# First mixer: a stacked low-rank product for the decays, and GpSimd for the weights' remainders

## The chip, the cores and the metric

One core of one Trainium2 chip runs the whole program in one launch. The metric is device microseconds of that core, the median of the runs shown. A core has five engines with queues of their own: TensorE (PE, with its weight loads as PEld), VectorE (DVE), ScalarE (ACT), GpSimd (POOL) and SyncE (SP, which issues most of the loads here). Within one queue, instructions start in order; a wait at the head of a queue holds all that stand behind it.

## The reference: what is computed

Two layers of a hybrid backbone over 768 tokens (512 latent and 256 context tokens) of width 1024, in float32. The change touches the first layer's mixer only, and there two things: the forget gates of the gated linear attention (GLA), and how projection weights are prepared.

```python
gq, gk, gv, gog, gz, aq, ak, av = _split(h @ w_in, EVEN_SIZES)   # gz: 32 columns, two directions of rank 16
...
for d, z in enumerate(jnp.split(gz, 2, axis=-1)):
    logit = (z @ gla_w_gate[d] + gla_b_gate[d]).astype(jnp.float32)
    g = _heads(jax.nn.log_sigmoid(logit) / GLA_GATE_TAU, GLA_HEADS)
    dirs.append(_directional_scan(q, k, v, g, n_ctx, reverse=(d == 1)))
```

For each direction, 16 columns of `gz` times a 16 x 256 matrix give 256 logits per token; their log-sigmoid is the log of the decay.

## The kernel before, in words

**How a product keeps float32 accuracy.** A matmul on plain float32 operands runs in several passes over the array, one on operands rounded to `fp32r` runs in one. The kernel therefore writes a large product X W as a sum of three one-pass products, with X = XH + XL and W = WH + WL (rounded part and remainder): `mm3` (line 812) issues H·H, H·L and L·H. ACT rounds a weight tile (`nc.scalar.copy`, line 803), and DVE makes its remainder, `raw - H` (line 804). Both stand in `split`, the inner function of `fetched` (lines 794 to 807), which first puts the load of the raw tile on SP's queue (line 799). The raw tiles have three buffers, `wH` and `wL` four each. `split` has a parameter `vector` for the engine of the subtraction; only the early columns of the first mixer (`weights`, line 2021) pass GpSimd, for tiles of 128 x 576. All others use DVE, in tiles of 128 x 1024. The two large feed-forward stages prepare their weights elsewhere (line 861) and are not touched.

**The first mixer** (`even_mixer`, from line 1115) multiplies the normed tokens by the columns of `w_in` in groups: `qk` (GLA's queries and keys, transposed), `nat` (values, output gates, attention's queries, keys and values), and `z` (the 32 columns of `gz` with 256 columns of attention's queries, computed first). Each of the groups qk0, qk1, v0, v1, q, kv, g0 and g1 loads two weight tiles of 128 x 1024, so there are sixteen of them.

**The decays.** ACT copies the 32 columns of each of six token tiles from PSUM to `zn` (line 1162). The generator `decays` (line 1173) turns them on PE into `zT`, 32 rows by 768 tokens, with a DVE copy out of PSUM (line 1179). `wg` holds both directions' 16 x 256 matrices, one below the other in 32 rows, with zeros elsewhere: a memset on GpSimd and two loads on SP (lines 1167 to 1170). `gla_gates` (line 1276) then does, for each half c of the columns, each token group (context, latent) and each direction, one plain float32 matmul of depth 32 (line 1285), and an Abs, Exp, Ln, min, subtract, Exp sequence on ACT and DVE (lines 1288 to 1293).

**The modulation vectors beside it.** In the same stretch DVE computes two pairs of modulation vectors out of 16 tiles of `mod_w` (`mod_vec`, from line 533): for each tile of 128 x 1024 two multiply-adds into accumulators `macc` (lines 553 and 555), whose loads (line 479) have three buffers of their own on SP's queue. After each half of the tiles PE sums the accumulators over the partitions (`mod_acc`), DVE copies the sums out (line 487), and PE turns them into columns.

**What sets the order.** On PE the order is written out by hand: strings of step names, each of which advances a generator by one step (`run`, line 1252), with the matmuls pinned to that order:

```python
run("qk0 e m qk0 e e v0 qk0 e e m qk0 e e m v0 e e m m q v0 m m v0 m m kv q m q m q m m m m m m m m m m qk1 kv m")
tp.release()
gp = self.open_pool("gla")
run("c0 l0 kv m c0 kv c0 v1 qk1 c0 p p qk1 c0 l0 p qk1 l0 c0 g0 qk1 l0 p c1 p v1 l0 p v1 l0 c1 p v1 l0 c1 l1 g1 g0 c1 g0 r0 c1 l1 r0 g0 l1")
```

Here `e` is `decays`, `m` is `mod_vec`, c0, l0, c1 and l1 are the chunked scans (`scan`, line 947), `p` is attention's normalisation and rotary step (`att_prep`, line 1334, which gives GpSimd a power and two multiplications per token tile, lines 686 and 1382), r0 and r1 the read-outs, x and y attention. The other engines' queues are ordered by the framework's planner, which places an instruction by its own costs when its inputs are due, so that order can shift when an instruction is moved or lengthened. The scans' memory (`gla`) takes the place of `gate`, which holds `zn`, `zT`, `wg`, `macc` and the tiles of `mod_w`; scans start when these are free.

Of the kernel before, what the change touches and what calls it, by code (L numbers as in the profile page):

```python
# [8 lines left out]
F32 = mybir.dt.float32  # L9
F32R = mybir.dt.float32r  # L10
# [3 lines left out]
ALU = mybir.AluOpType  # L14
# [3 lines left out]
P = 128  # L18
# [4 lines left out]
NT = SEQ + CTX  # L23
NTT = NT // P
# [9 lines left out]
class Split:  # L34


    def __init__(self, pool):
        self.pool, self.tiles = pool, None
# [26 lines left out]
class Forms:  # L65
# [29 lines left out]
    def split(self, n, f, i, m):  # L95
        H, L = (x[:, :, i : i + m] for x in self.tiles[n])
        self.net.nc.scalar.copy(H, f)
        self.net.mark = self.net.nc.vector.tensor_tensor(L, f, H.bitcast(F32), op=ALU.subtract)
# [218 lines left out]
class Net:  # L317
# [3 lines left out]
    def __init__(self, ctx, tc, I, out):  # L321
        self.tc, self.nc, self.I, self.out = tc, tc.nc, I, out
        tc.nc.scalar.preload_act_table_set("silu_and_others")
        self.side = 0
        self.whole = False
        self.pinned = False
        self.turns, self.steps, self.pair, self.casts, self.latest = [], [], [], [], []
        pool = lambda name, bufs=1, **k: ctx.enter_context(tc.tile_pool(name=name, bufs=bufs, **k))
        self.cst = pool("cst")
        self.wp = pool("wp")  # L330
        self.sm = pool("sm", 4)
        self.dr = pool("dr", space=bass.MemoryType.DRAM)
        self.ps = None
        self.banks(False)

    def pool(self, name, bufs=1):
        return self.tc.tile_pool(name=name, bufs=bufs, reuse_waits="tile")
# [456 lines left out]
    def fetched(self, src, k, n, raw=None):  # L794

        nc = self.nc
        raw = self.wp.tile([P, WU], F32, tag="raw", bufs=3, name="raw") if raw is None else raw
        m = k * n
        nc.sync.dma_start(out=raw[:, :m].rearrange("p (k n) -> p k n", k=k), in_=src)

        def split(pool=None, to=None, vector=nc.vector):
            H, L = to or [(pool or self.wp).tile([P, WU], F32R, tag=f"w{x}", bufs=4, name=f"w{x}") for x in "HL"]
            self.casts = self.casts[-1:] + [nc.scalar.copy(H[:, :m], raw[:, :m])]  # L803
            vector.tensor_tensor(L[:, :m], raw[:, :m], H[:, :m].bitcast(F32), op=ALU.subtract)  # L804
            return H[:, :m].rearrange("p (k n) -> p k n", k=k), L[:, :m].rearrange("p (k n) -> p k n", k=k)

        return split
# [307 lines left out]
    def even_mixer(self, h, mix, z):  # L1115
        nc, I = self.nc, self.I
# [8 lines left out]
        def q_part(n):  # L1125
            return natq.rearrange("p t (m n e) -> p t m n e", m=4, n=2)[:, :, :, n, :]
# [3 lines left out]
        gqk = [mixg.tile([P, NT], F32, tag=f"gqk{x}", bufs=1, name=f"gqk{2 * x}") for x in range(2)]  # L1130
        og = [p.tile([P, NTT, 256], F32, name=f"og{c}") for c, p in enumerate((mixg, mix))]
        tp = self.open_pool("gate")
        zn = tp.tile([P, NTT, 32], F32, name="zn")
        zT = tp.tile([32, NT], F32, name="zT")

        gq, gk, ends = {}, {}, {}
        def qk(c):
            Ws = {x: self.unit_cols(w, x * P) for x in (c, c + 2)}
            yield
            for x in (c, c + 2):  # L1140
                pt = self.mm_tile(f"gqk{x}")
                for g in groups:
                    self.gemm_T(pt, Ws[x], h, (g,))
                    if g is groups[-1]:
                        t = gqk[x // 2] if c == 0 else mixg.tile([P, NT], F32, tag=f"gqk{x // 2}", bufs=1, name=f"gqk{x}")
                        if x < 2:
                            nc.scalar.mul(t, pt[:, :NT], 0.125)
                            gq[c] = t
                        else:
                            nc.scalar.copy(t, pt[:, :NT])  # L1150
                            gk[c] = t
                    yield

        with self.behind():
            early = qk(0)
            next(early)
        rest = self.late_constants()
        self.pinned = True
        with self.tc.issue_after(self.casts[0].ins):
            for t0 in tiles:  # L1160
                for a, pt in enumerate(z(t0, 3)):
                    nc.scalar.copy(zn[:, t0 + a, :], pt[:, 0:32])
                    nc.scalar.copy(q_part(0)[:, t0 + a], pt[:, 32:288].rearrange("p (m e) -> p m e", m=4))
        self.pinned = False
        rest()

        wg = tp.tile([32, 2, 256], F32, name="wg")
        nc.gpsimd.memset(wg, 0.0)
        for d in range(2):
            nc.sync.dma_start(out=wg[16 * d : 16 * d + 16, d, :], in_=I["gla_w_gate"][0, d])  # L1170
        fs = [[], []]

        def decays():
            for g in range(0, NTT, 4):
                pt = self.tr_tile("zTp")
                n = min(4, NTT - g)
                for i in range(n):
                    self.tr(pt[0:32, i * P : (i + 1) * P], zn[:, g + i, :], self.ident)
                nc.vector.tensor_copy(zT[:, g * P : (g + n) * P], pt[0:32, : n * P])
            yield  # L1180
            for c in range(2):
                yield from self.gla_gates(mixg, tp, c, zT, wg, fs[c])
# [39 lines left out]
        def readout(c, tiles=tiles):  # L1222
# [18 lines left out]
            "g0": lambda: gates(0), "g1": lambda: gates(1), "p": lambda: self.att_prep(mixg, natq, natk),  # L1241
            "c0": lambda: job(0, 0), "l0": lambda: job(0, 1), "c1": lambda: job(1, 0), "l1": lambda: job(1, 1),
            "e": decays, "r0": lambda: (readout(0, (t,)) for t in tiles), "r1": lambda: (readout(1, (t,)) for t in tiles),
            "x": lambda: att.context(), "y": lambda: att.latent(ap),
            "t": lambda: self.gated_T(lambda t, hh: gv[:, t, hh * P : (hh + 1) * P], 4, R_GG, cat, ((4, 2), (0, 4))),
# [6 lines left out]
        def run(steps):  # L1252
            for x in steps.split():
                if x not in running:
                    running[x] = kinds[x]()
                next(running[x], None)
# [9 lines left out]
        mg.__exit__(None, None, None)  # L1266
        with self.pool("att") as ap:
            run("y x y g1 x y x y M x y")

            behind = {6: "t", 7: "r1", 9: "t", 10: "r1", 14: "M", 15: "r1", 16: "M", 17: "t", 19: "t", 22: "t", 24: "t", 26: "t", 29: "t"}  # L1270
            for i in range(3, 32 + 5):
                run("y " + behind.get(i, ""))
# [1012 lines left out]
```

## Time and profile before

| | |
|---|---|
| median of 3 runs (lowest, highest) | 1674.59 us (1673.91, 1675.4) |
| the profiled execution's own time | 1675.78 us |
| its span, first to last instruction | 1674.0 us |
| mean granted TensorE clock | 0.998 |
| busy: PE, DVE, ACT, POOL | 1644.8, 1311.1, 916.1, 129.4 us |

Times in the profile are microseconds from the start of the span. A row of a timeline or of the chain of waits gives a start, a time and the instructions merged in it (x4: four of them); a row of a group gives a count, the busy sum and the mean of one in nanoseconds, and the idle time before it. A plain float32 matmul stands as two records in this trace.

### The profile page before, as it was taken

What the parts mean: (1) busy time and instruction counts of PE and PEld (TensorE: products, weight loads), DVE (VectorE), ACT (ScalarE), POOL (GpSimd) and SP (SyncE); (2) the same over time, 40 slices, a digit from 0 to 9 for tenths busy, and PEclk for the clock granted to TensorE, in tenths of its full rate; (3) what the DMA queues carried; (4) which work ended last, traced back from release to release, by engine and by line L of the source; (5) the groups of instructions that cost most, each with busy time, mean ns of one, the idle gap of its engine ahead of it and who ended that gap; (6) DMA issues with size and microseconds to landing.
All of it is one profiled execution on the core that took longest, in us unless ns stands there. A gap on an engine that the chain in (4) does not pass through costs nothing.

```text
span 1674.0 us, 32524 instructions
## 1 busy us (share of the span) xinstructions
PE 1644.8 (98%) x13407; PEld 1481.1 (88%) x13407; DVE 1311.1 (78%) x2097; ACT 916.1 (55%) x1551; POOL 129.4 (8%) x139
## 2 busy tenths in 40 slices
PE   9999999999999999999999999999999999999998
PEld 7899987888999999998887888888888899999886
DVE  5999678976898988777668648788775599987887
ACT  5745567845544443446447436666664565555664
POOL 2004110011000000002102000000000100000310
PEclk9999999999999999999999999999999999999999
DMA  9641012164243445249525541121124333333973
GB/s 336 213 132 41 3 45 86 50 227 160 80 126 114 139 151 176 78 153 205 100 84 193 200 127 57 48 65 40 51 65 150 126 114 115 114 101 102 226 164 138
DMA packets 184736, 204.79 MB, mean 122 GB/s; under 512 B 7142, under 2 KB 141836, under 8 KB 184588
## 3 DMA queue, kind: packets, MB, share of 16 engines
q1 hardware_dynamic: 173996, 181.98, 34.7%
q0 software_dynamic: 9024, 17.30, 5.9%
q10 hardware_dynamic: 1568, 3.43, 0.6%
q8 instruction: 105, 1.72, 0.4%
q14 instruction: 43, 0.35, 0.1%
HBM read 193.23 MB, written 9.46 MB: 121 GB/s over the span
## 4 chain that ended last, share of the span: by engine, by line
PE 83%; DVE 8%; ACT 3%; DMA 3%; issue 2%; POOL 0%; SPq 0%; DVEq 0%; ACTq 0%; POOLq 0%
PE nat L355 12%; PE a L355 10%; PE ff L355 8%; PE E L355 7%; PE oproj L355 6%; PE x L355 6%; PE o L355 5%; PE D L355 4%; PE b L355 3%; PE fq L355 3%; PE gqk L355 2%; PE pearly L355 2%; PE q L355 2%; PE S L355 2%; PE poh L355 1%
## 5 line engine op out<-in xcount | busy, mean ns | idle before, releaser
L355 PE MATMUL nat<-wH,x 128*128 128x256 f32 (+2 forms) x968 | 226.7, 322 | 1.2 <-ACT x L2014 0.6
L860 ACT CAST wH<-raw 128x1024 fp32r<-128x1024 f32 x120 | 124.8, 1051 | 102.7 <-DVE raw L885 40.7
L355 PEld LDWEIGHTS nat<-wH,x 128*128 128x128 f32 x968 | 161.9, 190 | 19.5 <-ACT natq L1196 1.7
L861 DVE TENSOR_TENSOR wL<-raw,wH 128x1024 fp32r<-128x1024 f32 x120 | 145.7, 1222 | 23.6 <-ACT wH L860 23.3
L355 PE MATMUL nat<-wL,x 128*128 128x256 f32 (+2 forms) x484 | 153.5, 317 | 1.8 <-DVE wL L804 1.8
L804 DVE TENSOR_TENSOR wL<-raw,wH 128x1024 fp32r<-128x1024 f32 x79 | 95.8, 1222 | 50.6 <-ACT wH L803 49.8
L355 PE MATMUL ff<-x,wH 128*128 128x512 f32 (+1 forms) x512 | 127.6, 340 | 0.0
L686 POOL TENSOR_TENSOR rs<-ms,neghalf 128x1 f32<-128x1 f32 (+2 forms) x56 | 60.1, 1076 | 777.7 <-DVE ms L684 777.6
L803 ACT CAST wH<-raw 128x1024 fp32r<-128x1024 f32 x79 | 82.2, 1050 | 68.5 <-PE ff L355 19.7
L355 PE MATMUL oproj<-wH,x 128*128 128x512 f32 x320 | 102.2, 394 | 0.4 <-ACT x L1330 0.4
L355 PEld LDWEIGHTS nat<-wL,x 128*128 128x128 f32 x484 | 92.1, 190 | 7.8 <-DVE wL L804 2.7
L615 DVE SCALAR_TENSOR_TENSOR macc<-mraw,scT,macc 128x1024 f32<-128x1024 f32 x70 | 88.0, 1282 | 11.6 <-DMA mraw<-in_mod_w_dram 11.4
L355 PEld LDWEIGHTS ff<-x,wH 128*128 128x128 f32 x512 | 87.3, 190 | 10.0
L355 PE MATMUL x<-wH,two 128*128 128x512 f32 x280 | 90.5, 392 | 0.9 <-DVE y L1851 0.7
L1773 POOL DMA_DIRECT2D t<-in_ffn_w_down_dram x36 | 41.9, 1200 | 640.1 <-DVE t L1812 338.3
L1012 ACT COPY qkh<-arr 128x512 f32<-128x512 f32 x112 | 70.2, 641 | 36.6 <-DVE arr L1017 32.3
L355 PE MATMUL ff<-x,wL 128*128 128x256 f32 (+1 forms) x256 | 86.2, 337 | 0.0
L885 DVE TENSOR_TENSOR raw<-raw 128x512 f32<-128x512 f32 x120 | 82.8, 690 | 2.8
L1017 DVE TENSOR_TENSOR arr<-arr,f 128x512 f32<-128x512 f32 x112 | 74.4, 688 | 2.0 <-ACT qkh L1012 0.3
L355 PEld LDWEIGHTS oproj<-wH,x 128*128 128x128 f32 x320 | 59.9, 188 | 13.0 <-ACT x L1330 1.0
L355 PE MATMUL a<-T,wH 128*128 128x384 f32 (+1 forms) x320 | 70.5, 309 | 0.6 <-ACT qb L923 0.5
L355 PE MATMUL E<-T,wH 128*128 128x384 f32 (+1 forms) x320 | 70.4, 309 | 0.7 <-DVE go L938 0.7
(425 smaller groups left out, 4558.6 us busy)
## 6 DMA issues: line engine op xcount, KB each, us to landing
mraw<-in_mod_w_dram SPq DMA_DIRECT2D x80, 512.0 KB, 4.4
raw<-in_ffn_w_gate_dram SPq DMA_DIRECT2D x44, 512.0 KB, 3.9
raw<-in_ffn_w_up_dram SPq DMA_DIRECT2D x44, 512.0 KB, 4.9
raw<-in_odd_w_in_dram SPq DMA_DIRECT2D x40, 512.0 KB, 3.7
t<-in_ffn_w_down_dram POOLq DMA_DIRECT2D x30, 512.0 KB, 8.3
raw<-in_ffn_w_down_dram SPq DMA_DIRECT2D x28, 512.0 KB, 8.0
mraw<-in_mod_w_dram SPq DMA_DIRECT2D x32, 256.0 KB, 6.3
raw<-in_even_w_in_dram SPq DMA_DIRECT2D x16, 512.0 KB, 5.9
```

What stands on the lines that cost most here:

```text
L355: return self.pin(self.nc.tensor.matmul(*a, **k))
L615: nc.vector.scalar_tensor_tensor(a, u, w, a, op0=ALU.mult, op1=ALU.add)
L686: nc.gpsimd.tensor_tensor(rs, ms, self.neghalf.to_broadcast([P, w]), op=ALU.pow)
L803: self.casts = self.casts[-1:] + [nc.scalar.copy(H[:, :m], raw[:, :m])]
L804: vector.tensor_tensor(L[:, :m], raw[:, :m], H[:, :m].bitcast(F32), op=ALU.subtract)
L860: self.nc.scalar.copy(H, f)
L861: self.nc.vector.tensor_tensor(L, f, H.bitcast(F32), op=ALU.subtract)
L885: add = lambda o, x, y: nc.vector.tensor_tensor(o, x, y, op=ALU.add)
L1012: nc.scalar.copy(qkv[:, :, :, half, :], dst)
L1017: nc.vector.tensor_tensor(dst, dst, tb, op=ALU.mult)
L1773: add = lambda o, src: self.pin(nc.gpsimd.dma_start(out=o, in_=src, accum_op=ALU.add))
```

## The change

1. **Decays.** `zn` holds the 32 columns three times (ACT's copies are 96 wide). `decays` turns 96 columns at once; ACT copies all 96 rows out of PSUM, rounding them to `fp32r`, and DVE then overwrites rows 32 to 63 with the remainder of the rounding. `wg` is likewise 96 rows: the six small loads (two before) fill three copies of the matrices in `wr`, ACT rounds them, and GpSimd overwrites rows 64 to 95 with the remainder. So one one-pass matmul of depth 96 sums H·H, L·H and H·L; the eight matmuls of `gla_gates` are the same in number and shape, but for depth and type.
2. **Weights' remainders.** A new field `self.splitter` says which engine subtracts in `split` where no engine is passed. It is DVE, except from the start of the first mixer's groups until the first steps of latent attention, where it is GpSimd. That covers all sixteen weight tiles of 128 x 1024.

```diff
+        self.splitter = self.nc.vector
...
-        def split(pool=None, to=None, vector=nc.vector):
+        def split(pool=None, to=None, vector=None):
...
-            vector.tensor_tensor(L[:, :m], raw[:, :m], H[:, :m].bitcast(F32), op=ALU.subtract)
+            (vector or self.splitter).tensor_tensor(L[:, :m], raw[:, :m], H[:, :m].bitcast(F32), op=ALU.subtract)
...
-        zn = tp.tile([P, NTT, 32], F32, name="zn")
-        zT = tp.tile([32, NT], F32, name="zT")
+        zn = tp.tile([P, NTT, 3, 32], F32, name="zn")
+        zT = tp.tile([96, NT], F32R, name="zT")
...
+        self.splitter = nc.gpsimd
         with self.behind():
             early = qk(0)
...
-                    nc.scalar.copy(zn[:, t0 + a, :], pt[:, 0:32])
+                    nc.scalar.copy(zn[:, t0 + a], pt[:, 0:32][:, None, :].to_broadcast([P, 3, 32]))
...
-        wg = tp.tile([32, 2, 256], F32, name="wg")
-        nc.gpsimd.memset(wg, 0.0)
+        wr = tp.tile([96, 2, 256], F32, name="wr")
+        wg = tp.tile([96, 2, 256], F32R, name="wg")
+        nc.gpsimd.memset(wr, 0.0)
         for d in range(2):
-            nc.sync.dma_start(out=wg[16 * d : 16 * d + 16, d, :], in_=I["gla_w_gate"][0, d])
+            for x in range(3):
+                nc.sync.dma_start(out=wr[32 * x + 16 * d : 32 * x + 16 * d + 16, d, :], in_=I["gla_w_gate"][0, d])
+        nc.scalar.copy(wg, wr)
+        nc.gpsimd.tensor_tensor(wg[64:96], wr[64:96], wg[64:96].bitcast(F32), op=ALU.subtract)
...
-                    self.tr(pt[0:32, i * P : (i + 1) * P], zn[:, g + i, :], self.ident)
-                nc.vector.tensor_copy(zT[:, g * P : (g + n) * P], pt[0:32, : n * P])
+                    self.tr(pt[0:96, i * P : (i + 1) * P], zn[:, g + i].rearrange("p x j -> p (x j)"), self.ident)
+                tok = slice(g * P, (g + n) * P)
+                nc.scalar.copy(zT[:, tok], pt[0:96, : n * P])
+                nc.vector.tensor_tensor(zT[32:64, tok], pt[32:64, : n * P], zT[32:64, tok].bitcast(F32), op=ALU.subtract)
...
             run("y x y g1 x y x y M x y")
+            self.splitter = nc.vector
```

## The prediction

> **What bounds the kernel now.** I read the page first, then the busy times by stretch through the first mixer, then the chain of waits there.
>
> ```profile
> span 1674.0 us, 32524 instructions
> PE 1644.8 (98%) x13407; PEld 1481.1 (88%) x13407; DVE 1311.1 (78%) x2097; ACT 916.1 (55%) x1551; POOL 129.4 (8%) x139
> ```
>
> ```profile
> core 0: us, PE busy (x) PEld busy (x) DVE busy (x) ACT busy (x) POOL busy (x), PEclk, DMA share, GB/s
> 60.00:75.00 15.00, 15.00 (x80) 11.58 (x81) 14.50 (x19) 13.07 (x22) 0.00 (x0) 1.00 0.80 243
> 90.00:105.00 15.00, 15.00 (x125) 14.03 (x124) 14.35 (x14) 3.19 (x5) 0.00 (x0) 1.00 0.68 218
> 120.00:135.00 15.00, 15.00 (x289) 14.19 (x288) 14.97 (x38) 11.21 (x27) 8.44 (x6) 1.00 0.03 6
> ```
>
> PE is full in all three stretches, so a PE microsecond saved here shortens the span until some wait takes it back. DVE is nearly as full (14.5, 14.35 and 14.97 of 15): it is the engine that can take it back. GpSimd is idle until the scans. The chain of waits shows the decays' products and the place where PE needs DVE's long sum:
>
> ```profile
> 50.91 5.49 PE gqk L355 x24
> ...
> 59.92 1.06 PE logit L355 x4
> 60.97 5.68 PE gqk L355 x24
> 66.65 1.91 PE logit L355 x4
> 68.56 3.07 PE gqk L355 x24
> 71.63 1.05 PE logit L355 x4
> ...
> 78.63 1.91 PE logit L355 x4
> ...
> 111.25 0.99 PE mod_acc L355 x8
> ```
>
> **Part 1: the products.** The eight plain float32 matmuls hold PE for 1.06 + 1.91 + 1.05 + 1.91 = 5.93 us. In one pass they should go at the rate of their neighbours gqk: 5.68 / 24 = 0.237 us for 512 columns, 3.07 / 24 = 0.128 us for 256 (depth 128 there, 96 here; I take it as the same). Four of each make 1.46 us. PE saves 5.93 - 1.46 = **4.5 us**. No other engine has to be faster for it.
>
> What feeds them gets longer:
>
> ```profile
> 58.75 0.41 DVE L1179 COPY zT<-zTp 32x256 f32<-32x256 f32 x1
> ```
>
> ```profile
> 45.66 0.83 SPq L1170 DMA_DIRECT2D wg<-in_gla_w_gate_dram  x2
> 46.53 0.42 SPq L479 DMA_DIRECT2D mraw<-in_mod_w_dram  x1
> ```
>
> The six transposes stream the identity as before, so I cost their wider weights at nothing. The last zT copy ends at 59.16, 0.76 us before the first product. Now an ACT copy comes first and DVE's subtraction of about the same size second, so the product may wait: nothing at best, some 0.6 us of copy plus one held-up DVE instruction (below, 2.2 us) less the 0.76 at worst, about 2 us. The six wider zn copies on ACT add a fraction of a microsecond ahead of the queue's idle time. Four more small loads take 2 x 0.83 = 1.7 us of SP's queue; the mod_w load behind them slips by that, and it is the third tile of a sum that DVE, not the load, paces. The memset, ACT's rounding and GpSimd's remainder for wg have 14 us from the loads to the first product. A PE wait of up to 2 us at 59.92 is paid only if nothing later is later still.
>
> **Part 2: sixteen remainders move.** What DVE does until 111 us:
>
> ```profile
> L804 DVE TENSOR_TENSOR wL<-raw,wH x10: 1215/1224/1226, 47.9 to 112.9; 128x1024 fp32r<-128x1024 f32 x10
> ```
>
> ```profile
> L555 DVE SCALAR_TENSOR_TENSOR macc<-mraw,scT,macc x28: 1194/1280/1286, 54.2 to 106.1; 128x1024 f32<-128x1024 f32 x28
> ```
>
> ```profile
> 106.05 1.28 DVE L555 SCALAR_TENSOR_TENSOR macc<-mraw,scT,macc 128x1024 f32<-128x1024 f32 x1
> 107.25 0.17 DVE L662 TENSOR_TENSOR gc<-modcol,col 128x16 f32<-128x16 f32 x1
> 110.82 1.23 DVE L804 TENSOR_TENSOR wL<-raw,wH 128x1024 fp32r<-128x1024 f32 x1 [3.40 <-ACT wH L803]
> ```
>
> ```profile
> 47.94 2.36 DVE L804 TENSOR_TENSOR wL<-raw,wH 128x1024 fp32r<-128x1024 f32 x2
> ```
>
> The second modulation sum ends at 106.05 + 1.28 = 107.33; PE asks for it at 111.25, a slack of 3.9 us. A PE that is 4.5 us earlier asks at 106.8: already with DVE unchanged it would wait 0.5 us. So the second half of the change decides. Eight of the ten remainders in this stretch lie ahead of that sum (one stands at 110.82 and the last at 112.9); a remainder takes 2.36 - 1.22 = 1.14 us of DVE's queue. Without them, and if nothing else happened, the sum would end 8 x 1.14 = 9.1 us sooner and PE would keep its 4.5 us.
>
> GpSimd's price per tile, from its own remainders and multiplications:
>
> ```profile
> L804 POOL TENSOR_TENSOR wL<-zraw,wH 128x576 fp32r<-128x576 f32 x4 | 5.7, 1417 | 22.7 <-ACT wH L803 22.7
> ```
>
> ```profile
> 126.82 1.04 POOL L1382 TENSOR_TENSOR natq<-natq,rs 128x512 f32<-128x512 f32 x1
> ...
> 141.56 0.75 POOL L1382 TENSOR_TENSOR natk<-natk,rs 128x128 f32<-128x128 f32 x2
> ```
>
> In proportion to 576 columns, 1024 take 1.417 x 1024 / 576 = 2.52 us. With the slope of the multiplications, (1.04 - 0.375) / 384 columns, they take 1.417 + 448 x 0.00173 = 2.19 us. I take 2.35, twice DVE's time. [...]
>
> That alone would be nearly harmless. The tightest of the sixteen is the first: DVE starts it at 47.94, GpSimd would end it at 50.3, and the first gqk product that reads it is the third after 50.91. PE has no use for the second before 60.97, nor for the others as early as they are made. But the trace shows the two engines stopping each other. DVE's row and GpSimd's at the same moment, then a second pair:
>
> ```profile
> 126.19 0.41 DVE L1017 TENSOR_TENSOR arrg<-arrg,glaf 128x256 f32<-128x256 f32 x1
> 126.52 0.61 DVE L997 COPY_PREDICATED CTg<-masks,pcg 128x64 f32<-128x64 uint8 x4
> 127.04 1.10 DVE L1017 TENSOR_TENSOR arrg<-arrg,glaf 128x256 f32<-128x256 f32 x1
> ```
>
> ```profile
> 247.24 1.14 DVE L1235 SCALAR_TENSOR_TENSOR gvo<-gvo,og 128x512 f32<-128x512 f32 x1
> ...
> 250.59 0.69 DVE L1235 SCALAR_TENSOR_TENSOR gvo<-gvo,og 128x512 f32<-128x512 f32 x1
> ```
>
> ```profile
> 247.22 0.61 POOL L164 CAST kH<-kH 64x512 fp32r<-64x512 f32 x1
> ```
>
> The same multiplication takes 0.41 us alone and 1.10 when GpSimd's natq (126.82 to 127.86) is running: taking its own 0.41 off its end at 128.14, it got going at 127.73, when GpSimd was all but done. The multiply-add at 247.24 lost 0.45 us to a cast of 0.61. The masked copies, which read PSUM, went on at their pace. So a DVE instruction with two inputs in SBUF stands still while GpSimd streams, and the 28 multiply-adds of L555 (mraw and macc) are of that kind. [...]
>
> So a remainder on GpSimd holds DVE for 2.35 - 0.13 = 2.2 us in place of 1.14: 1.08 us more. Eight make 8.6, and wg's remainder (32 rows by 512 columns: 1.417 x 512 / 576 = 1.26, less 0.13) makes 9.7. Not all of it lands: DVE idles some 4% of these stretches (14.35 of 15), and about twice that share should go to instructions that read PSUM, like the masked copies; an estimate, so I take 1.4 off. The sum ends 8.3 us later, at 115.6, and PE, which stands still for it whatever it saved before, is 115.6 - 111.25 = **4.4 us later** than now. A wait at 59.92 is swallowed by this one. Behind the waiting products on PE's queue stands everything that follows; SP's weight loads wait for raw tiles that GpSimd frees, at about the same times as now, since it starts when ACT's rounding is done and not in DVE's turn.
>
> Ends of this sum: with 2.19 us per tile the extra is 0.92 x 8 + 1.0 = 8.4, and if half of it falls into gaps PE ends 0.3 us later than now; with 2.52 it is 1.25 x 8 + 1.2 = 11.2, nothing hidden, and PE ends 7.3 us later. After 112 us eight remainders are left. Two fall beside 110 us, where DVE now idles 3.4 us, and g1's two after the scans' densest part; the four of v1 and g0 fall among the scans:
>
> ```profile
> 135.33 0.75 DVE L1017 TENSOR_TENSOR arrg<-arrg,glaf 128x256 f32<-128x256 f32 x2
> 136.00 1.22 DVE L804 TENSOR_TENSOR wL<-raw,wH 128x1024 fp32r<-128x1024 f32 x1
> ```
>
> ```profile
> 138.88 0.59 PE knpg L358 x4
> ```
>
> PE turns the result of that scan 2.8 us after DVE made it; two longer remainders cost 2.2, so I take 0 here, and at most 4 x 1.08 = 4.3 less 2.8, 1.5 us. That gives +0.3 to +8.8 for this case.
>
> **The sum.** The profiled execution took 1675.78 us, 1.78 over its span and 1.19 over the median. With 4.4 us more it would be 1680.2; against the median, 1674.59 + 4.4 = **1679.0 us**.
>
> **The rivals.** *PE keeps its saving.* GpSimd's tiles fall where DVE reads PSUM or idles, or the planner spreads DVE's work so that the sum still ends by 106.8 us. For it: DVE is relieved of 9.1 us, and GpSimd does nothing else here. Against it: 28 multiply-adds of 1.28 us fill most of the 52 us, so GpSimd nearly always meets one. 1674.6 - 4.5 = 1670.1 us; it decides where the hold is under DVE's own 1.14 us a tile. *Even.* Half the hold is hidden: about 0.5 us a tile, the sum ends near 111.3, PE neither gains nor loses: 1674.6 us, with 1671.3 to 1677.9 counted here. *The scans stall as well.* The remainders of v1 and g0, GpSimd's powers and multiplications for attention queued behind them, and DVE at 14.97 of 15 use up the 2.8 us: 4.4 + 1.5 plus as much again from attention's normalisation, 1682 us. *The products don't get faster* (the depth of 96 taking several passes): then PE is at 111.25 as before and the sum still ends at 115.6; the same 1679, so the time can't tell it, the rows of logit can.
>
> **How the numbers follow.** About 0.2% (3.3 us) is what a measurement of this kernel can tell from no change. Forecast 0.45, of which 0.07 lies less than 3.3 us up; scans as well 0.12; even 0.21; PE keeps its saving 0.22. That the products don't get faster (0.05) is held within the forecast, as it gives the same time. So slower 0.38 + 0.12 = 0.50, same 0.07 + 0.21 = 0.28, faster 0.22. The likeliest case's own range is 1674.9 to 1683.4; leaving the faster case out would leave out more than 2 in 10, so the range reaches from just under it, 1669.6, to 1683.6.
>
> **What would show it.** In the changed profile: logit rows of about 0.13 and 0.24 us each, 1.5 us in all; L804 on GpSimd sixteen times more, 2.2 to 2.5 us each or longer where it first waits for DVE; L555 with a mean well over 1280 ns, single ones over 3 us; PE idle ahead of the second mod_acc, released by macc, and little idle ahead of it elsewhere. The prediction is wrong if L555 keeps its 1.28 us beside GpSimd, if the second sum ends before 108 us, or if PE does not wait at that mod_acc.

## The result, and the profile after

The changed kernel takes 1692.49 us (median; 1692.28 to 1694.35), the kernel before beside it 1674.77: the ratio is 1.0109, with an interval of 1.0097 to 1.0121. The change is slower by 17.7 us. The forecast had the direction, but its 4.4 us are a quarter of it, and 1692.5 lies 9 us above its range.

The profiled execution took 1692.44 us, its page begins so:

```profile
span 1690.7 us, 32542 instructions
PE 1646.0 (97%) x13399; PEld 1484.7 (88%) x13399; DVE 1322.0 (78%) x2081; ACT 916.7 (54%) x1554; POOL 170.3 (10%) x156
```

PE's busy sum rose by 1.2 us although eight products became cheaper. So its instructions got slower somewhere, and the rest of the 16.7 us of span is standing still. The busy times by stretch show where (duration, PE, PEld, DVE, ACT, POOL, then the granted clock):

```profile
60.00:75.00 15.00, 9.74 (x37) 8.07 (x38) 14.90 (x14) 6.71 (x13) 6.36 (x2) 0.77 0.66 220
105.00:120.00 15.00, 9.48 (x80) 8.87 (x83) 13.02 (x13) 2.23 (x3) 2.34 (x1) 0.95 0.42 135
120.00:135.00 15.00, 15.00 (x106) 13.34 (x106) 12.92 (x27) 11.01 (x24) 2.38 (x1) 0.83 0.27 80
150.00:165.00 15.00, 13.32 (x224) 11.49 (x228) 11.51 (x27) 3.91 (x10) 7.58 (x6) 0.89 0.37 107
```

Before, PE was full and at clock 1.00 in each of the four; the two that the prediction doesn't show:

```profile
105.00:120.00 15.00, 15.00 (x126) 13.95 (x125) 11.52 (x25) 9.96 (x20) 0.00 (x0) 1.00 0.28 80
150.00:165.00 15.00, 15.00 (x400) 14.20 (x400) 14.90 (x37) 11.13 (x24) 5.90 (x4) 1.00 0.01 4
```

Now it is idle for five of fifteen microseconds in two of them, and the granted clock of the four is 0.77 to 0.95. PE's five longest waits from 45 to 240 us, beside one of 1.1 us that both kernels have:

```profile
PE logit L356 <- DVE zT L1187: 5.6, 1, 5.6
PE gcT L359 <- DVE gc L663: 3.4, 1, 3.4
PE modT L359 <- DVE modrows L488: 2.1, 1, 2.1
PE knpg L359 <- DVE arrg L1018: 1.6, 1, 1.6
PE pcg L356 <- DVE glaf L1019: 1.5, 1, 1.5
```

All five are released by DVE, and the kernel before has none of them. What DVE does meanwhile, in its timeline (start, duration, line, operation, in brackets the idle time before):

```profile
50.67 0.25 DVE L420 COPY col<-pt_rows 128x86 f32<-128x86 f32 x1 [2.80 <-PE pt_rows L359]
50.95 4.39 DVE L453 TENSOR_TENSOR lb_tmp<-col 128x16 f32<-128x16 f32 x1
...
59.50 4.56 DVE L556 SCALAR_TENSOR_TENSOR macc<-mraw,scT,macc 128x1024 f32<-128x1024 f32 x2
64.09 1.02 DVE L1187 TENSOR_TENSOR zT<-zTp,zT 32x512 fp32r<-32x512 f32 x2
...
116.18 3.23 DVE L556 SCALAR_TENSOR_TENSOR macc<-mraw,scT,macc 128x1024 f32<-128x1024 f32 x1
```

GpSimd's remainders in the same trace, a timeline row, then the group (count, least, median and greatest duration in ns):

```profile
50.55 4.75 POOL L805 TENSOR_TENSOR wL<-raw,wH 128x1024 fp32r<-128x1024 f32 x2
```

```profile
L805 POOL TENSOR_TENSOR wL<-raw,wH x16: 2341/2398/3382, 47.7 to 199.5; 128x1024 fp32r<-128x1024 f32 x16
```

The clearest row is L453: a maximum over 16 columns that took 0.18 us before lasts 4.39 us, because two GpSimd tiles run from 50.55 to 55.30. The first logit waits for zT, zT stands on DVE's queue behind two multiply-adds of which one is held, and PE starts the products at 65.25 in place of 59.92. Behind that wait comes what the forecast did not have, in the chain of waits:

```profile
65.25 0.77 PE logit L356 x2
66.02 7.70 PE gqk L356 x24
...
119.64 0.37 PE gcT L359
120.02 1.94 PE mod_acc L356 x8
```

The 24 gqk products took 5.68 us before, now 7.70; the eight of mod_acc took 0.99, now 1.94. They are the same instructions at a lower clock: 0.61 over 66 to 72 us, 0.50 over 120 to 122, where the kernel before has 1.00.

**The account.** Four marks on PE's queue, before and after: the second mod_acc from 111.25 to 120.02, **8.8** us late; the modT behind it

```profile
118.03 0.60 PE L358 MATMUL modT<-ident,modrows 128*128 128x128 f32 x4
```

```profile
129.18 0.60 PE L359 MATMUL modT<-ident,modrows 128*128 128x128 f32 x4
```

11.15 us late; a group of 48 products behind the densest part of the scans

```profile
166.29 5.75 PE nat L355 x48
```

```profile
182.98 5.75 PE nat L356 x48
```

16.7 us late; and the end of the span, 16.7 us late. So 8.8 us come with DVE's second sum, 2.4 from there to modT, where PE waits for nothing and only runs slower (the clock is at 0.50 until 125.2), and 5.5 among the scans. Those 48 products serve below as the mark of where a run stands against the kernel before.

### The profile page after: what moved, and what is told of

Its sections match the earlier page's. It is cut to its first block, busy times and chain, and to the rows that moved or that the text cites. A ratio compares the mean times of both kernels' runs of the same rounds, so it can differ in the third digit from the quotient of the medians.

```text
span 1690.7 us, 32542 instructions
## 1 busy us (share of the span) xinstructions
PE 1646.0 (97%) x13399; PEld 1484.7 (88%) x13399; DVE 1322.0 (78%) x2081; ACT 916.7 (54%) x1554; POOL 170.3 (10%) x156
## 3 DMA queue, kind: packets, MB, share of 16 engines
q10 hardware_dynamic: 1568, 3.43, 0.6%
## 4 chain that ended last, share of the span: by engine, by line
PE 75%; DVE 12%; DMA 5%; ACT 3%; issue 3%; POOL 1%; SPq 0%; DVEq 0%; ACTq 0%; POOLq 0%
PE a L356 10%; PE nat L356 8%; PE ff L356 8%; PE E L356 7%; PE x L356 6%; PE oproj L356 6%; PE o L356 4%; PE D L356 4%; PE b L356 3%; PE fq L356 3%; DMA mraw<-in_mod_w_dram 2%; PE pearly L356 2%; PE q L356 2%; PE S L356 2%; PE poh L356 1%
## 5 line engine op out<-in xcount | busy, mean ns | idle before, releaser
L862 DVE TENSOR_TENSOR wL<-raw,wH 128x1024 fp32r<-128x1024 f32 x120 | 145.6, 1220 | 23.3 <-ACT wH L861 22.8
L805 DVE TENSOR_TENSOR wL<-raw,wH 128x1024 fp32r<-128x1024 f32 x63 | 76.3, 1222 | 43.7 <-ACT wH L804 43.0
L356 PE MATMUL E<-x,wH 128*128 128x384 f32 (+1 forms) x320 | 70.6, 310 | 0.0
```

The costliest lines, as they stand in the source:

```text
L356: return self.pin(self.nc.tensor.matmul(*a, **k))
L805: (vector or self.splitter).tensor_tensor(L[:, :m], raw[:, :m], H[:, :m].bitcast(F32), op=ALU.subtract)
L862: self.nc.vector.tensor_tensor(L, f, H.bitcast(F32), op=ALU.subtract)
```

## The experiments

The theories as I held them when the runs were sent: *Theory 1*, a GpSimd subtraction of two SBUF tiles holds DVE while it runs, and DVE's second sum sets PE's time. *Theory 2*, PE's standing still costs clock as well. *Theory 3*, the scans lose by themselves. The rivals are in the expectations.

### 1. The products alone

```diff
-        self.splitter = nc.gpsimd
         with self.behind():
```

> Only the decays' stacked product, with its feed (zn, zT, wg) and GpSimd's one remainder for wg; all sixteen remainders of 128x1024 back on DVE. Theory 1 (GpSimd's tiles hold DVE, and that alone turned the change into a loss): PE keeps most of its 4.5 us, less about 0.5 us of wait for the modulation sum: about 1670.7 us, 3.5 to 4.2 under the kernel before; no PE wait at the first logit of more than 1 us. Rival A (the feed of the stacked product, that is six loads, a memset, the rounding and a subtraction more, is what delays the first logit by 5 us): the first logit still starts 3 us or more late, and the time is 1675 to 1680.

Measured: 1675.4 against 1674.62 us, ratio 1.0004 (0.9996 to 1.0013): no difference. Theory 1's 1670.7 is missed by 4.7 us, and the time lies inside rival A's 1675 to 1680. Rival A falls all the same, by its own sign: the first logit waits 0.3 us here, so the feed of the stacked product is not what delays it. The products did their part:

```profile
L356 PE MATMUL logit<-zT,wg x8: 282/376/397, 60.0 to 75.3; 96*128 96x256 f32 x4, 96*128 96x512 f32 x4
```

The last starts at 75.3 in place of 80.0. But at the second mod_acc PE stands before each half for DVE's accumulator (the rows below). It is 5.0 us ahead of the kernel before when it starts gcT (105.94 against 110.97) and 3.4 us ahead when the sum is done (108.76 against 112.17). Another 1.4 us go among the scans, and at the mark it is 2.0 us ahead (164.32 against 166.29):

```profile
106.44 1.05 PE L356 MATMUL mod_acc<-macc,one 128*32 128x512 f32 x4 [0.23 <-DVE macc L556]
107.78 1.05 PE L356 MATMUL mod_acc<-macc,one 128*32 128x512 f32 x4 [0.28 <-DVE macc L556]
```

### 2. GpSimd's remainders alone

zn, zT and wg as in the kernel before, the splitter as in the changed one.

> Only the sixteen remainders on GpSimd; the decays as in the kernel before. Theory 1 (DVE's second modulation sum sets PE's time, so what the products save is spent waiting): the sum still ends at 117 to 119.5, PE reaches it with a shorter wait, and the time is 1687 to 1691, at most the changed kernel's, though the products are slow again. Rival B (the two effects add up): 1692.5 + 4 = 1696.5 us. If the first logit is not late here, the wait at it came of the two parts together.

Measured: 1693.26 us, ratio 1.0112 (1.0092 to 1.0131). That is 0.8 us over the changed kernel and 2.3 over theory 1's range. Its four runs go from 1689.46 to 1697.32, so the time decides neither for theory 1 nor for rival B. The profiled execution (1690.43) is even 0.75 us ahead of the changed kernel's at the mark (182.23 against 182.98), with the old, slow products: no sign that the products bring their 4 us while GpSimd makes the remainders. Theory 1's reason for it is only half right, since PE does not wait at the sum here. It is late already from the first logit, and loses most among the scans (waits from 45 to 240 us):

```profile
PE logit L356 <- DVE nlb L469: 4.1, 1, 4.1
PE knpg L359 <- DVE arrg L1018: 3.1, 1, 3.1
```

The logit waits 4.1 us with the old, plain zT copy as well (nlb is DVE's next instruction behind that copy). So that wait came from GpSimd's part, not from the two parts together.

### 3. Is it the hold, or GpSimd's slower delivery?

```diff
+            if vector is None and self.splitter is nc.gpsimd:
+                spare = self.mixg.tile([P, WU], F32, tag="spare", bufs=1, name="spare")
+                nc.gpsimd.tensor_tensor(spare[:, :m], raw[:, :m], H[:, :m].bitcast(F32), op=ALU.subtract)
+                vector = nc.vector
             (vector or self.splitter).tensor_tensor(L[:, :m], raw[:, :m], H[:, :m].bitcast(F32), op=ALU.subtract)
```

> DVE makes all remainders that are used; GpSimd makes the sixteen of 128x1024 as well, into a spare tile that nobody reads. So no product and no DVE instruction waits for GpSimd's result. Theory 1 (a GpSimd tensor_tensor in SBUF holds DVE's two-input instructions while it runs): DVE has its own 1.14 us a tile and the hold of 2.2 besides, the second modulation sum ends 6 to 9 us later than in the changed kernel, and the time is 1697 to 1702. Rival D (what cost the time was that GpSimd delivers each remainder later, and the weight buffers come free later): the time is that of the products alone, 1670 to 1673.

Measured: 1702.58 us, ratio 1.0168 (1.0154 to 1.0182), 10 us over the changed kernel. That is 0.6 us over theory 1's range and 30 over rival D's. Nobody needs a result of GpSimd's, and it is the slowest of all runs: rival D falls. (A raw tile still comes free only when GpSimd has read it, but PE's waits are all for DVE, none for a weight.) The waits of PE, 45 to 135 us:

```profile
PE logit L356 <- DVE zT L1191: 8.2, 1, 8.2
PE mod_acc L356 <- DVE macc L556: 4.5, 2, 3.2
```

### 4. Reading or writing?

```diff
-            (vector or self.splitter).tensor_tensor(L[:, :m], raw[:, :m], H[:, :m].bitcast(F32), op=ALU.subtract)
+            if vector is None and self.splitter is nc.gpsimd:
+                nc.gpsimd.memset(L[:, :m].bitcast(F32), 0.0)
+            else:
+                (vector or self.splitter).tensor_tensor(L[:, :m], raw[:, :m], H[:, :m].bitcast(F32), op=ALU.subtract)
```

> The changed kernel, but GpSimd writes zeros into the sixteen remainder tiles in place of the subtraction, so it streams the same number of elements out and reads nothing; the sixteen weights' remainders are left out of the result. Theory 1 (it is GpSimd's reading from SBUF that holds DVE): no multiply-add of L556 over about 1.4 us beside these writes, DVE relieved of all sixteen, and the time is 1668 to 1672. Rival F (any GpSimd instruction holds DVE for as long as it runs): a write of 1024 columns takes about 1.04 us (twice the 0.52 of the 512 columns of wr), about what DVE's own subtraction took, multiply-adds of 2.0 to 2.4 us stand beside the writes, and the time is 1673 to 1676.

Measured: 1672.76 us, ratio 0.9988 (0.9979 to 0.9998). The time lies between the two expectations; the rows do not. The writes wait for no rounding, so they come earlier than the subtractions did: four of the sixteen (at 60.53, 69.50, 86.30 and 87.74) run beside multiply-adds, six in all. None of these is held (the groups of L806 on GpSimd and L556 on DVE):

```profile
L806 POOL MEMSET wL<- x16: 951/952/964, 41.8 to 176.2; 128x1024 f32 x16
```

```profile
L556 DVE SCALAR_TENSOR_TENSOR macc<-mraw,scT,macc x28: 1275/1280/1285, 59.5 to 103.9; 128x1024 f32<-128x1024 f32 x28
```

Of 28 multiply-adds none is over 1.285 us; in the changed kernel the longest took 3.426. Rival F falls for the instructions with two inputs: GpSimd's subtractions, which read two tiles, held them here, and its writes of 0.95 us did not. One instruction that scales and shifts a single tensor did take 1.19 us beside a write, where the kernel before takes 0.54 for it, and PE waited 0.8 us for what follows from it. That is one case, and its cause was not tested:

```profile
45.24 1.19 DVE L2027 TENSOR_SCALAR xa<-xT,aff,modcol 128x512 f32<-128x512 f32 x1
```

```profile
45.20 0.95 POOL L806 MEMSET wL<- 128x1024 f32 x1 [1.55 <-PE nat L356]
```

From the first logit to the mark PE waits nowhere, and at the mark it is 4.4 us ahead (161.88). That is what the products are worth when DVE gets out of the way; DVE is relieved of all sixteen subtractions here as well.

### 5. Shorter pieces

```diff
+            cuts = [(0, m // 2), (m // 2, m)] if vector is None and self.splitter is nc.gpsimd else [(0, m)]
+            for a, b in cuts:
+                (vector or self.splitter).tensor_tensor(L[:, a:b], raw[:, a:b], H[:, a:b].bitcast(F32), op=ALU.subtract)
```

> The changed kernel with each of the sixteen remainders as two instructions of 512 columns on GpSimd. Theory 1 (the two engines take turns, and the sum of both is what counts): the holds are shorter and twice as many, 1.1 to 1.2 us each, and the time is within 3 us of the changed kernel's, 1689.5 to 1695.5. Rival G (it is the length of one hold that hurts, a short instruction that PE needs standing behind a long one): the zT subtraction and the sums come sooner, and the time is 1680 to 1687.

Measured: 1688.3 us, ratio 1.008 (1.0063 to 1.0097), 4 us under the changed kernel and between the two expectations. The longest multiply-add is 2.322 us in place of 3.426:

```profile
L556 DVE SCALAR_TENSOR_TENSOR macc<-mraw,scT,macc x28: 1268/1277/2322, 60.0 to 113.0; 128x1024 f32<-128x1024 f32 x28
```

The first logit is hardly earlier, 0.6 us (64.68), though gcT starts 3.7 us sooner (115.97 in place of 119.64). So the length of one hold matters somewhat, the total more: a mixed result.

### 6. Which tiles cost what

A word in the string of steps switches the splitter at qk1: GpSimd from there on (e4_late), or up to there (e5_early).

> GpSimd makes the remainders from qk1 on (the last eight tiles: qk1, v1, g0, g1); DVE makes the first eight (qk0, v0, q, kv). The stacked product stays. Theory 3 (the scans' stage loses by itself, about a third of the whole loss, since each tile there holds DVE while PE waits for what the scans need of it): first logit not late (under 1 us of wait), PE at the second mod_acc about 2 us later than with the products alone, 4 to 6 us more among the scans: 1679 to 1682 us. Rival E (the scans have the room that the forecast gave them, and everything is lost ahead of 121 us): 1675 to 1677, that is the products alone and at most 1.5 us.

> GpSimd makes the first eight remainders (qk0, v0, q, kv), DVE the last eight (qk1, v1, g0, g1). The stacked product stays. Theory 3: the first logit is about 5 us late, the clock drops behind it, the second modulation sum ends 1 to 2 us sooner than in the changed kernel since qk1's tiles no longer hold it, and the scans lose no more than with the products alone: 1683 to 1687 us. Rival E (all of the loss is made ahead of 121 us by the eight early tiles): 1690 to 1693.

Measured: 1678.69 us for the late eight (ratio 1.0027, 1.0016 to 1.0039) and 1684.23 for the early eight (1.0061, 1.0046 to 1.0076). The late half is 0.3 us under theory 3's range, the early half inside it; rival E falls on both counts. At the mark the late eight are 4.5 us behind the products alone (168.82 against 164.32), the early eight 8.55 behind (172.87). Together that makes 13.0, while the changed kernel is 18.7 behind (182.98): the two halves hurt each other, and the remaining 5.6 us are only there when both are moved. With the early eight alone PE does not wait at the sum at all, since qk1's tile no longer holds it at the end; being late from the first logit, and a wait of 2.1 us at modT, is then what stays. With the late eight alone PE waits 2.2 us at the second mod_acc and 1.4 among the scans.

### 7. The clock

First, PE's waits of the changed kernel filled with products nobody reads, then a pause put into the kernel before.

```diff
+    def busy(self, n):
+        pt = self.sc_tile("busy", self.side)[:, :P]
+        for _ in range(n):
+            self.mm(pt, self.ident, self.ident, start=True, stop=True)
...
-        run("qk0 e m qk0 e e v0
+        run("qk0 e m qk0 w16 e e v0
...
+                self.busy(11)
                 rows()
```

> The changed kernel, and 34 products of the identity with itself whose result nobody reads, put on PE's queue into its three longest waits: 16 ahead of the first logit, 7 ahead of modT, 11 ahead of gcT. They are made to fit into the waits. Theory 2 (after PE stands still the granted clock falls to half, and the products behind each wait are slow for some 6 us): the clock stays at 1.00 behind the first and the third wait, and the time falls by 4 to 6 us, to 1686.5 to 1688.5. Rival C (the clock is a sign of the waits and costs nothing by itself, because what follows waits for DVE anyway): the time stays at 1692 to 1693, with longer waits behind.

Measured: 1688.39 us, ratio 1.0083 (1.0067 to 1.0098): 4.1 us back, as theory 2 had it, but not cleanly. The first wait is a fair comparison, the logit starts at 65.29 as against 65.25, and behind it the clock is whole (first row; 0.61 from 66 to 72 us in the changed kernel) and the gqk products take their 5.5 us. But the framework's planner then ordered DVE's work otherwise, and the third logit waited 4.3 us for DVE to read the PSUM tile before it, with the clock down in that stretch (second row):

```profile
65.00:71.00 6.00, 5.71 (x26) 4.82 (x27) 5.94 (x8) 3.31 (x7) 0.61 (x1) 1.00 0.92 277
75.00:90.00 15.00, 11.08 (x67) 10.70 (x68) 15.00 (x17) 12.31 (x23) 3.48 (x1) 0.77 0.55 176
```

So one wait's clock was bought back and another wait took its place. Hence the opposite experiment, without any of the change:

```diff
+        self.mm(pt, self.ident, self.ident, start=True, stop=True)
+        t = pool.tile([P, P], F32, name="pause")
+        self.nc.scalar.copy(t, pt)
+        for _ in range(n):
+            self.nc.scalar.copy(t, t)
+        pt = self.sc_tile("resume", self.side)[:, :P]
+        self.mm(pt, t, self.ident, start=True, stop=True)
...
+                self.pause(pool, 14)
                 rows()
```

> The kernel before, with nothing of the change, and PE held up once: ahead of gcT, at 111.2 us, it waits for a chain of fifteen small ACT copies, some 3 to 4.5 us long; DVE's sum is done by then. Theory 2 (standing still costs PE the clock as well): the granted clock falls to half behind the pause, mod_acc and the products behind it take about 2.4 us more than in the kernel before, and the time is the pause plus 2 to 3 us, 1679.5 to 1682. Rival C (only the pause counts): the eight mod_acc products take 0.99 us as before and the time is 1677.5 to 1679.

Measured: 1683.59 us, ratio 1.0056 (1.0043 to 1.007). The time fits neither range, because the chain of copies was longer than I took it for: PE stood for 6.0 us, and gcT starts 6.8 us late (117.97 against 111.14). The rows behind it are what decides:

```profile
117.17 0.80 PE resume L355 x2
117.97 0.21 PE gcT L358
118.18 1.87 PE mod_acc L355 x8
120.05 7.24 PE nat L355 x48
```

The same three took 0.11, 0.99 and 5.96 us in the kernel before: 0.10 + 0.88 + 1.28 = 2.3 us more, without a wait among them. With the 6.8 us that makes 9.1, and the run is 9.4 us slower. The granted clock is the reason:

```profile
120.00:122.00 2.00, 2.00 (x13) 2.00 (x10) 1.89 (x5) 0.96 (x4) 0.00 (x0) 0.50 0.00 0
122.00:124.00 2.00, 2.00 (x16) 2.00 (x14) 2.00 (x6) 2.00 (x5) 0.00 (x0) 0.77 0.04 8
```

In the changed kernel the same stretch, second mod_acc to modT, lost 2.4. Rival C falls. By the last two rows the clock is back at 122.92 (0.77 of the stretch's clock is 0.92 us at half and 1.08 at full), 5.7 us after PE resumed. In the changed kernel PE's wait of 1.6 us for knpg, which ends at 151.58, is followed by this:

```profile
152.00:156.00 4.00, 3.90 (x21) 3.89 (x21) 2.23 (x12) 1.96 (x7) 2.35 (x2) 0.57 0.50 137
```

A mean of 0.57 over four microseconds is 3.4 us at half. The length of the wait alone does not decide it: behind the wait of 2.1 us at modT (109.82) the clock stays at 1.00 in the changed kernel, and behind the same wait in e5_early it is at half for 3.4 us (0.66 over 110 to 115 us). So it is behind the waits of 2.2 and 1.4 us of e4_late (0.72 over 109 to 115 us, 0.66 over 158 to 163).

### 8. Can the products be made to pay?

Experiment 4 showed 4.4 us ahead at the mark when DVE is free. Two cheaper ways: ACT makes the four multiplications that begin the sums, and the tiles of mod_w get a fourth buffer.

```diff
-                        nc.vector.tensor_scalar(a, u, w, None, op0=ALU.mult)
+                        nc.scalar.mul(a, u, w)
...
-        mods = self.mod_vec(tp, ((0, ((2, 0), (2, 1)), (2, R_NQM)), (0, ((3, 0), (3, 1)), None)), tp, 3, 4)
+        mods = self.mod_vec(tp, ((0, ((2, 0), (2, 1)), (2, R_NQM)), (0, ((3, 0), (3, 1)), None)), tp, 4, 4)
```

The first edit by itself (e9), the second by itself (e12), and both (e11):

> The products alone, and the four multiplications that begin the modulation sums (L554, 0.98 us each on DVE) made by ACT, which is idle for much of 90 to 105 us. Theory 4 (with the products alone it is DVE's second sum that takes back what PE saves): the sum ends about 2 us sooner, the 1.4 us that PE lost at the second mod_acc go away, and PE is 4 to 5 us early at 121 us; the time is 1671 to 1673. Rival H (what is saved ahead of the scans is taken back by the scans, whose inputs come from DVE at their own pace): PE is early at 121 us and no longer at 160 us, and the time is 1674 to 1675.5, that of the kernel before.

> The products alone, with four buffers in place of three for the tiles of mod_w. In the two runs with the products alone SP's loads of mod_w waited for buffers that DVE's multiply-adds free, and the last tiles of the second sum came late. Theory 4 (the sum's loads take back what the products save at the second mod_acc): the loads start one tile sooner, the wait at the second mod_acc is under 0.5 us, PE is 4 to 5 us early at 121 us and 3 at 230 us, and the time is 1671.5 to 1673, measurably under the kernel before. Rival H (every saving ahead of the scans and the feed-forward layer is taken back there by DVE): 1673.5 to 1675.

> The same with ACT making the four first multiplications of the sums as well. Theory 4: no wait at the second mod_acc, PE 4.5 to 5 us early at 121 us, the time 1671 to 1672.5. Rival H: 1673.5 to 1675.

Measured: 1673.93, 1674.46 and 1673.98 us; ratios 0.9999, 0.9999 and 0.9998, each with an interval that includes 1. None is measurably faster. The times are rival H's, the first within 0.1 us, and theory 4's ranges are missed by 0.9 to 1.5 us. With ACT alone the mark is at 163.19, and the sum still comes late: in the chain of waits its last part begins with a load of mod_w that had to wait for a buffer (94.15 to 100.06).

With both, the wait at the second mod_acc is gone and the mark stands at 162.38, 3.9 us ahead. That is near theory 4's 4.5 to 5 and against rival H, which had the scans take it back; but the time did not follow. So either the lead is over-read or it is lost later. The kernel before and the version with both edits were run once more, unchanged:

> The kernel before once more, unchanged, for a second profile. Theory 5 (the steps of one kernel start at the same times in every execution, to a few tenths, up to about 300 us, and executions differ later): the second mod_acc starts at 111 us within 0.5, og at 215 us within 0.5, and what differs from the first profile comes behind 600 us. Rival I (the first profile was of a slow execution from the start): the starts at 111 and 215 us are 1 us or more earlier.

> The products alone with four buffers and ACT's first multiplications, once more, unchanged. Theory 5: PE is again 4 us ahead of the kernel before at 230 us, and the lead at the end is another one than the 3.7 us of the first profile, 0 to 3 us, lost behind 600 us. Rival I: the lead at 230 us is itself different by 1 us or more from the first profile's.

Measured: 1674.5 and 1674.16 us (ratios 1.0003 and 0.9996, both intervals include 1). Where the products of oproj first start in three profiles (the kernel before, the same again, both edits; the last two times of a group's row are its first and last start), and the spans:

```profile
L355 PE MATMUL oproj<-wH,x x320: 388/389/504, 334.7 to 1328.5; 128*128 128x512 f32 x160
```

```profile
span 1671.6 us, 32524 instructions
...
L355 PE MATMUL oproj<-wH,x x320: 388/389/503, 334.5 to 1327.4; 128*128 128x512 f32 x160
```

```profile
span 1670.3 us, 32525 instructions
...
L356 PE MATMUL oproj<-wH,x x320: 388/389/503, 330.8 to 1323.8; 128*128 128x512 f32 x160
```

At 335 us two executions of one kernel stand within 0.3 us of each other (both edits again: 331.1, span 1669.7), and the lead of 3.4 to 3.9 us is real. At the end the two executions of the kernel before differ by 2.4 us (1674.0 and 1671.6), and the lead is anything from 1.3 to 4.3 us, by which two are compared. Theory 5 holds up to 335 us, and rival I, with its 1 us or more, falls; of the lead at the end, 0 to 3 us by theory 5, only some of the comparisons fit. In the medians of 11 runs 0.3 and 0.7 us are left, which cannot be told from nothing. In these profiles the lead is not lost on PE: the last product of oproj still starts 4.7 and 3.6 us earlier (1323.8 against 1328.5 and 1327.4). But both profiled executions of both edits were faster than their medians, by 1.9 and 2.6 us (1672.07 and 1671.52), so no profile shows an execution that lost it. What takes it there stays open.

## Why the prediction was right and wrong

**Right: the products.** Eight matmuls at 0.13 and 0.24 us, PE 4.7 us earlier in experiment 1 (4.5 forecast). **Right: GpSimd's price**, 2.40 us a tile (2.35 forecast). **Right: the mechanism**, DVE's two-input instructions standing still while GpSimd makes a remainder (L453 4.39 us in place of 0.18, a multiply-add up to 3.426 in place of 1.28), and a PE that waits for DVE's second sum. The holds even sum to the forecast; the groups of 45 to 120 us in the changed kernel,

```profile
L556 DVE SCALAR_TENSOR_TENSOR macc<-mraw,scT,macc 128x1024 f32<-128x1024 f32 x28 | 47.0, 1725 | 1.5 <-DMA mraw<-in_mod_w_dram 1.5
L453 DVE TENSOR_TENSOR lb_tmp<-col 128x16 f32<-128x16 f32 x1 | 4.4, 4387 | 0.0
```

and of the multiply-adds in the kernel before,

```profile
L555 DVE SCALAR_TENSOR_TENSOR macc<-mraw,scT,macc 128x1024 f32<-128x1024 f32 x28 | 34.7, 1277 | 0.7 <-DMA mraw<-in_mod_w_dram 0.7
```

make 47.0 - 34.7 = 12.3; with 4.2 for L453 (0.18 before) and 1.1 for L459 (0.17 to 1.26), 17.6 us; the forecast's 8 x 2.2 + 1.1 less the hidden 1.4 is 17.3.

**Wrong, 4.4 us: the end of the sum.** Forecast 115.6, it came at 119.41 (116.26 + 3.15 in the chain). The step that failed is "without them ... the sum would end 8 x 1.14 = 9.1 us sooner": the first two tiles' time was freed where DVE had nothing else to do. It idles 2.80 us ahead of L420 now, 0.49 before, so 2.3 of the 9.1 were worth nothing. Waiting for mod_w loads cost 0.8 more (1.5 against 0.7), and waiting for the logits cost 0.8 less (0.5 against 1.3). With 0.3 of longer holds that is 2.6 of the 3.8; the other 1.2 is spread over many short rows and was not traced. The further 0.6 from there to mod_acc is gc, and gcT at the lower clock (0.50 over 119 to 120 us).

**Wrong, 2.4 us, and 1.8 of the 5.5 below: no term for the clock.** The sum took PE's instructions at their old durations behind every wait. The pause of experiment 7 shows this price without the change, 2.3 us. "A wait at 59.92 is swallowed" was right for the changed kernel's mod_acc, where PE still stood 3.4 us, but it was sized at 2 us and came to 5.6, and with the early tiles alone nothing swallowed it.

**Wrong, 5.5 us: "I take 0 here, and at most ... 1.5 us" for the scans.** The 2.8 us of room was read at one place, in a kernel whose DVE was on time. Now the scans' arrg and attention's natk meet GpSimd's tiles, as here (DVE's timeline, then GpSimd's and PE's):

```profile
146.57 2.45 DVE L1388 TENSOR_TENSOR natk<-natk,rope 128x64 f32<-128x64 f32 x1
148.94 3.12 DVE L1018 TENSOR_TENSOR arrg<-arrg,glaf 128x256 f32<-128x256 f32 x2
```

```profile
146.55 4.69 POOL L805 TENSOR_TENSOR wL<-raw,wH 128x1024 fp32r<-128x1024 f32 x2
```

```profile
151.58 0.98 PE L359 MATMUL knpg<-ident,arrg 128*128 128x128 f32 x4 [1.60 <-DVE arrg L1018]
```

A pair of multiplications that took 0.75 us takes 3.12, and PE stands 1.6 us for it. It starts knpg 12.8 us late (138.82 before) and pdg, the next product but for one group of gqk, 14.6 us late (156.85 against 142.27): 1.8 us more without a wait, at the half clock that experiment 7 shows behind knpg (0.57 over 152 to 156 us). Two later waits, for glaf and CTg, cost 1.5 and 0.2. So of the 5.5 us 3.3 are waits and 1.8 the clock; the other 0.4 are short gaps. The rival "the scans stall as well" was the nearest of the four, and it put 1.5 plus as much again where 5.5 fell.

Together 4.4 + 4.4 + 2.4 + 5.5 = 16.7 us, the difference of the spans.

The rival "PE keeps its saving" had the right test, the hold against DVE's own 1.14 us a tile, but even with the sum's holds gone (experiment 4) the time fell by 1.8 us, not by 4.5. With DVE unchanged the forecast had PE wait 0.5 us at the sum; experiment 1 lost 1.6 there, and 1.4 among the scans, which the forecast did not have.

## What to carry to other kernels

Work moved from a busy engine to an idle one is only moved if the idle one doesn't hold the busy one while it works: price the hold it puts on the busy engine, on the shortest instruction that someone waits for, and not only on the long ones. Time freed on an engine counts only where that engine has something to do at that moment. A wait on a full TensorE cost its own length here and, in the four places priced above (behind waits of 1.6 to 6.0 us), 1.8 to 2.4 us lost to the half clock besides; behind a wait of 2.1 us in the changed kernel it cost no clock. And slack read off one place of a trace is gone once the engine that made it is late.

## What the runs showed of the hardware

GpSimd's remainders of 2.40 us, which read two SBUF tiles, held DVE instructions with two SBUF inputs: a multiply-add of 1.28 us took up to 3.43, and an instruction of 16 columns that takes 0.18 us stood through two of them in a row (4.39). Of six multiply-adds beside GpSimd's writes of 0.95 us none was held (none of all 28 took over 1.285). The granted clock went from 1.00 to 0.50 during the changed kernel's wait of 3.4 us, and in e10_pause it was back 5.7 us after the end of a wait of 6.0; it went to 0.50 behind a wait of 1.6 us too, and of two waits of 2.1 us at the same place in two kernels behind one only. The changed kernel's stretches at 0.50, the one at its end aside, are 63.8 to 70.6, 118.4 to 125.2 and 152.5 to 155.9 us, that is 6.8, 6.8 and 3.4 us; in e6_hold the clock is 0.66 over 60 to 75 us and again over 120 to 135. And two executions of one kernel, equal within 0.3 us at 335 us, differed by 2.4 us at the end.
